# A broadcast through TensorE without a diagonal, and two conversion steps placed anew, in a fused decoder layer

## The chip, the cores and the metric

The kernel runs on one core of one Trainium2 chip. The metric is the time of one execution on the device in microseconds (us), taken as the median of several runs.

A core has five engines with a queue of instructions each: TensorE (PE, matrix products, with PEld for its weight loads), VectorE (DVE), ScalarE (ACT), GpSimd (POOL) and SyncE (SP), which here only issues transfers. They wait for each other by semaphores. Products are summed in PSUM; all other tiles lie in SBUF.

## The reference

One layer of a decoder, with x of 1024 positions by 1024 features, all in float32:

```python
h = rmsnorm(x)
q, k, v, su, sv, g_a, g_b = split(h @ w_in)
y_att = sliding_window_attention(q, k, v, ...)     # window 128, 8 heads of 64, ALiBi, sinks
y_sgu = chunked_spatial_gating(su, sv, ...)
x = x + (sigmoid(g_a) * (y_att @ w_oa) + sigmoid(g_b) * (y_sgu @ w_ob)) @ w_out
x = x + down(silu(conv_g) * conv_v)                # conv over positions of up(rmsnorm(x)), d_ff 2816
```

Two places matter here: the factor 1/rms of each position that the two `rmsnorm` of whole rows need (`rmsnorm(y)` is y times 1/sqrt(mean(y*y) + 1e-6), times a gain).

## The kernel before

Activations are held transposed: features on the 128 partitions, the 1024 positions along a row. So 1/rms differs from column to column, and to multiply by it the kernel needs a tile `rstd_b` of 128 x 1024, in which every partition holds the same 1024 numbers.

*High and low parts.* Most products use a faster form of float32 that keeps fewer bits. Each operand is split: a high part (rounded copy, on ACT, line L75) and a low part (operand minus high part, a subtraction on DVE or POOL), and each product is three: high by high, high by low, low by high. The names end in h and l, or have index 0 and 1.

*Blocks.* From the gates on, a product of 1024 x 1024 operands is put together from seven products of half-size blocks (a Strassen-like scheme). Left blocks (weights) are A11, A12, S1, S2, S3, S4, A22; right blocks (activations) are B11, B21, B22, T1, T2, T3, T4. `prod(o, l, r)` issues the 12 matrix products of one block product (L1014). The sums of weights for S2 and S4 are made on POOL into `lr` (`sums_r`, L608) and split by `split_r` into a tile named AX, the high part on ACT and the low part on POOL (L974).

*Order.* In the stages around the change each engine executes in the order in which the code issues (`manual_schedule`); nothing is reordered. An instruction that waits holds up all behind it on its engine.

*The first place* (L297 to L403, some 30 to 54 us into the run). Behind the k and v projection, `p_ssq` sums the squares of the columns, `rsqrt_cols` turns them into `rstd` (128 x 8: eight columns of 128 positions each; scale and offset on DVE, L115, then a power on POOL, L116). A diagonal tile `diag` is built on DVE from `ident` and `rstd` (L322). Later `rms_rows` multiplies ones (as weights) by the diagonal on PE (L123), which leaves each position's factor in all 128 partitions, and ACT copies the result into `rstd_b` (L125). It is called for the two halves one after the other, between the products of the q projection. Beside this, POOL takes two more powers (`krs`, L116), DVE makes `kr` (L331) and PE transposes it (L338).

*The second place* (L1432 to L1552, some 556 to 601 us). Here the gated MLP begins. `first_pair` computes the first of 22 pairs of column blocks of `up`, and the second pair's first product (`fast_pair(1)`) is interleaved. The last output tile has just been finished, so the sum of squares of the new x is completed here too: `late_split` makes the high and low parts of T2 (low on DVE) and of T4 (low on POOL, both L1445), ACT squares the last tile (L1459), DVE adds these to `sq2` (L1460), and `ssq_cols` lets PE sum the columns (L1340), and makes of them the ratio of the new 1/rms to the one that the activations were already multiplied by (L1344 to L1347, the power on POOL, L116). A diagonal of the ratio is built on DVE (L1349). Meanwhile PE does A22·T4 of the first pair and A11·B11 of the second. Then `rms()` issues the products with the diagonal (L123) and the copies into `rstd_b` (L125), and scales the first pair. The copy `x1` of A11·B11 (named x1f in the profile, L1509) must be taken before A12·B21 is added to the same accumulator.

Of the kernel before, what the change touches and what calls it, by code (L numbers as in the profile page):

```python
# [10 lines left out]
F = mybir.dt.float32  # L11
# [3 lines left out]
ALU = mybir.AluOpType  # L15
# [26 lines left out]
def body(ctx, tc, nc, a):  # L42
    L, H = slice(0, 512), slice(512, 1024)
# [6 lines left out]
    def nm(s):  # L50
        uid[0] += 1
        return f"{s}_{uid[0]}"
# [8 lines left out]
    def PS(s):  # L61
        pools_ = psum["P"]
        pools_.append(pools_.pop(0))
        return pools_[-1].tile([128, 1024], F, tag="P", name=nm(s))

    def PH(s):
        if psum.get("H") is None:
            return PS(s)[:, 0:512]
        return psum["H"].tile([128, 512], F, tag="H", name=nm(s))
# [4 lines left out]
    def copy_hi(dst, src, scale=1.0):  # L74
        return nc.scalar.activation(dst, src, AF.Copy, scale=scale)  # L75
# [26 lines left out]
    ident = base.tile([128, 128], F, name="ident")  # L102
    ones = base.tile([128, 128], F, name="ones")
    mh05 = base.tile([128, 16], F, name="mh05")
    rstd_b = base.tile([128, 1024], F, name="rstd_b")
    rstd = base.tile([128, 8], F, name="rstd")
# [6 lines left out]
    def rsqrt_cols(dst, ss, n, width):  # L113

        nc.vector.tensor_scalar(dst, ss, 1.0 / width, EPS, op0=ALU.mult, op1=ALU.add)  # L115
        return nc.gpsimd.tensor_tensor(dst, dst, mh05[:, :n], op=ALU.pow)  # L116

    msk = base.tile([128, 4, 128], U8, name="msk")

    def rms_rows(pb, diag, hs=(0, 1)):  # L120

        for h, p in zip(hs, pb):
            nc.tensor.matmul(p, ones, diag[:, h * 4:(h + 1) * 4, :], start=True, stop=True)  # L123
        for h, p in zip(hs, pb):
            nc.scalar.copy(rstd_b[:, h * 512:(h + 1) * 512], p)  # L125

# [48 lines left out]
    pa = pa_cm.__enter__()  # L175
# [30 lines left out]
    for k in range(8):  # L206
# [8 lines left out]
        for s in range(8):  # L215
            o = pkv[s // 4][:, (s % 4) * 256:(s % 4 + 1) * 256]
            c = slice(s * 128, (s + 1) * 128)
# [25 lines left out]
    def q_proj(n):  # L243
        half, b = divmod(n, 8)
        w = wq[half]
        p = PH("pq")[:, 0:256]
        c = slice(b * 128, (b + 1) * 128)
        for k in range(8):
            mm3(p, hx(0, k, c), hx(1, k, c), w[:, 0, k, :], w[:, 1, k, :], k == 0, k == 7)
        st[("pq", n)] = p  # L250


    def q_sq(n):
        p = st.pop(("pq", n)).rearrange("p (h d) -> p h d", d=64)
        sq = qp.tile([128, 4, 64], F, tag="qsq", name=nm("qsq"), bufs=2)
        nc.scalar.activation(sq, p, AF.Square)
        st[("q", n)] = [p, sq]
# [42 lines left out]
    for s in range(8):  # L300
        nc.tensor.matmul(p_ssq[:, 2 * s:2 * s + 2], sqsum[:, s * 128:(s + 1) * 128], ones[:, 0:2],
                         start=True, stop=True)
# [9 lines left out]
    for h in range(2):  # L312
# [5 lines left out]
    nc.vector.tensor_tensor(kss3, kss3, rstd2.unsqueeze(2).to_broadcast([128, 8, 2]), op=ALU.mult)  # L318
    rsqrt_cols(krs[:, 0:8], kss[:, 0:8], 8, 64)
    rsqrt_cols(krs[:, 8:16], kss[:, 8:16], 8, 64)  # L320
    diag = pa.tile([128, 8, 128], F, tag="sq", name="diag")
    nc.vector.tensor_tensor(diag, ident.unsqueeze(1).to_broadcast([128, 8, 128]),  # L322
                            rstd.unsqueeze(2).to_broadcast([128, 8, 128]), op=ALU.mult)
    q_sq(0)
    q_sq(1)

# [60 lines left out]
    q_split(0)  # L387
    q_trans(1)
    q_split(1)
    rms_rows([PH("rb")], diag, (0,))  # L390
    q_proj(3)
    k_trans(1)
    rms_rows([PH("rb")], diag, (1,))
    q_sq(2)
    v_split()
    q_ms(2)
# [320 lines left out]
    rb = sg.tile([128, 512], F, name="rb")  # L717
# [620 lines left out]
    def ssq_cols(p):  # L1338
        for s in range(8):
            nc.tensor.matmul(p[:, 2 * s:2 * s + 2], pools["sq2"][:, s * 128:(s + 1) * 128], ones[:, 0:2],  # L1340
                             start=True, stop=True)
        pool = pools["fp"]
        ss = pool.tile([128, 8], F, name="ss8b")
        nc.vector.tensor_copy(ss, p[:, 0:16].rearrange("p (s two) -> p s two", two=2)[:, :, 0])  # L1344
        rsqrt_cols(ss, ss, 8, D)
        nc.vector.reciprocal(rstd, rstd)
        nc.vector.tensor_tensor(ss, ss, rstd, op=ALU.mult)  # L1347
        diag = pool.tile([128, 8, 128], F, tag="ac", name="diag2", bufs=2)
        nc.vector.tensor_tensor(diag, ident.unsqueeze(1).to_broadcast([128, 8, 128]),  # L1349
                                ss.unsqueeze(2).to_broadcast([128, 8, 128]), op=ALU.mult)  # L1350
        return diag

    class Pair(Blocks):

# [66 lines left out]
    lefts = [Left(a["wup"][2 * i], a["wup"][2 * i + 1], i) for i in U_ORDER]  # L1421
# [10 lines left out]
    def first_pair():  # L1432
        w, nx = lefts[0], lefts[1]
        z = PS("pz"), PS("pz")
        q, q2 = Pair(0, w.w, z[::-1]), Pair(1, nx.w)
        xu = pools["fp"].tile([128, 1024], F, tag="h", name="xu", bufs=2)
        x7, u2 = xu[:, L], xu[:, H]
        x1 = pools["fp"].tile([128, 512], F, tag="ac", name="x1", bufs=2)

        def late_split(n, r, eng):  # L1440
            comb[n] = Y(n, R, [128, 2, 4, 512])
            for k in range(0, 4, 2):
                src, h = pools[r][:, k:k + 2, :], comb[n][:, 0, k:k + 2, :]
                copy_hi(h, src)
                eng.tensor_tensor(comb[n][:, 1, k:k + 2, :], src, h.bitcast(F), op=ALU.subtract)  # L1445

        q.prod(q.v1, "A11", "B11")
        nc.scalar.copy(x1, q.v1)
        w.split_r(0)
        nx.load_p()  # L1450
        q.prod(q.g0, "A12", "B21")
        late_split("T2", "raw2", nc.vector)
        nx.load_q()
        nx.load_s3()
        q.prod(q.g1, "S1", "T1")
        nc.scalar.copy(u2, q.g1)
        late_split("T4", "raw4", nc.gpsimd)
        for c, p in zip((L, H), late["px"]):
            nc.scalar.activation(p, late["ac"][:, c], AF.Square)  # L1459
            nc.vector.tensor_tensor(pools["sq2"][:, c], pools["sq2"][:, c], p, op=ALU.add)  # L1460
        q.prod(q.v0, "S3", "T3")
        nc.scalar.copy(x7, q.v0)
        nx.split_p()
        nx.split_s3()
        nc.vector.tensor_tensor(x7, x7, u2, op=ALU.add)
        q.prod(q.g1, "S4", "B22", more=True)
        nc.vector.tensor_tensor(q.g0, q.g0, x1, op=ALU.add)
        q.prod(q.v1, "S2", "T2", more=True)
        pb = q2.zv
        diag = ssq_cols(pb)  # L1470
        nx.sums_r()
        nx.split_q()
        lefts[2].load_p()
        q.prod(q.v0, "A22", "T4", more=True)
        nc.scalar.copy(u2, q.v1)
        q.u2 = u2
        nx.split_r(1)
        nc.vector.tensor_tensor(q.v1, u2, x7, op=ALU.add)
        nc.vector.tensor_tensor(q.v0, u2, q.v0, op=ALU.add)

        def rms():

            rms_rows([pb[:, L], pb[:, H]], diag)
            q.scale(q.zv)
            q.last_sum()

        pools["ft_cm"] = tc.tile_pool(name="ft", bufs=1, reuse_waits="tile")
        return q, q2, rms

    def fast_pair(n, prev, q, hooks, rms=None):  # L1490

        nx = lefts[n + 1] if n + 1 < NPAIR else None

        def temp(t, p="ft"):
            return pools[p].tile([128, 512], F, tag=t, name=nm(t), bufs=2 if p == "ft" else 1)

        if rms:
            x1 = temp("x1f", "wx")
        else:
            prev.last_sum()  # L1500
            prev.tap_v()
            x1, x7, q.u2 = temp("x1"), temp("x7"), temp("u2")
        q.prod(q.g0, "A11", "B11")
        if nx:
            nx.load_q()
            nx.load_s3()
        else:
            hooks[2]()
        nc.scalar.copy(x1, q.g0)  # L1509
        if rms:  # L1510
            rms()
            pools["fp_cm"].__exit__(None, None, None)
            pools["ft"] = pools["ft_cm"].__enter__()
            x7, q.u2 = temp("x7"), temp("u2")
            prev.tap_v()
            q.prod(q.g0, "A12", "B21", more=True)
        prev.tap_g()
        prev.conv()
        q.prod(q.v0, "S3", "T3")
        if nx:  # L1520
            nx.split_s3()
        nc.scalar.copy(x7, q.v0)
        if not rms:
            q.prod(q.g0, "A12", "B21", more=True)
        if rms:
            nx.split_p()
        prev.tanh()
        if not rms:
            prev.gated()
        q.prod(q.g1, "S1", "T1")  # L1530
        if nx and not rms:
            nx.split_p()
        nc.vector.tensor_tensor(x7, x7, q.g1, op=ALU.add)
        if rms:
            prev.gated()
        prev.stores()
        if nx:
            nx.sums_r()
        if n + 2 < NPAIR:
            lefts[n + 2].load_p()  # L1540
        q.prod(q.v0, "A22", "T4", more=True)
        if nx:
            nx.split_q()
            nx.split_r(n + 1)
        else:
            hooks[0]()
        q.prod(q.v1, "S2", "T2")
        q.sums(x1, x7, q.v0)
        if not nx:
            hooks[1]()  # L1550
        q.prod(q.g1, "S4", "B22", more=True)
        return q  # L1552
# [282 lines left out]
```

## Time and profile before

| | us |
|---|---|
| Median of 3 runs | 1198.88 |
| Lowest, highest | 1198.02, 1199.2 |
| Profiled execution, from its first to its last instruction | 1196.2 |
| Median above that span | 2.7 |

| Engine | Busy, share of the span |
|---|---|
| PE | 99% |
| DVE | 74% |
| POOL | 48% |
| ACT | 45% |

A row of a timeline or of the chain has the start in us from the begin of the span, the duration, the engine, the line, the operation, the tiles written and read, shapes and a count; in brackets how long the engine had been idle before, and what ended that. Durations include the time in which an instruction that had been started was held up. For the profiled execution the profile gives its span, and what lies around it is taken as the difference to the median. The mean granted clock of PE was 0.999 of full speed.

### The profile page before, as it was taken

To read this page: it belongs to the slowest core of one execution; us is meant where nothing else is said; L and a number is where in the kernel's file an instruction comes from. 1 tells how busy PE (TensorE), PEld (TensorE's weight loads), DVE (VectorE), ACT (ScalarE), POOL (GpSimd) and SP (SyncE) were. 2 spreads that over 40 slices of the span, in tenths; PEclk is the share of its full clock that TensorE was granted. 3 is DMA by queue.
4 is the path that set the end of the run, shared out by engine and by line. 5 is a ranking of instruction groups with operands and counts; after the bars stand their busy time and mean duration, and the time that the engine had idled before them with its cause. 6 is when DMAs were issued, how large, how long until landed. Compare 5 with 4: busy or idle time off the path is not lost.

```text
span 1196.2 us, 15840 instructions
## 1 busy us (share of the span) xinstructions
PE 1183.4 (99%) x5866; PEld 1002.4 (84%) x5866; DVE 881.4 (74%) x1028; ACT 543.0 (45%) x832; POOL 574.4 (48%) x365
## 2 busy tenths in 40 slices
PE   9999999999999999999999999999999999999998
PEld 9889989988888888888788888888888888888886
DVE  8788975755638565668887788878788788775674
ACT  8555567644335222234444444444444445434331
POOL 2467685588668222344866575656657541000000
PEclk9999999999999999999999999999999999999999
DMA  7010143037786997342143342423333268975471
GB/s 283 23 53 19 54 139 126 11 122 271 237 308 206 358 320 273 128 166 98 45 150 108 104 136 102 149 89 123 109 129 124 87 205 290 370 235 194 150 238 61
DMA packets 79133, 191.27 MB, mean 160 GB/s; under 512 B 8912, under 2 KB 9168, under 8 KB 79056
## 3 DMA queue, kind: packets, MB, share of 16 engines
q1 hardware_dynamic: 79056, 190.26, 46.2%
q8 instruction: 46, 0.75, 0.3%
q14 instruction: 31, 0.25, 0.1%
HBM read 139.63 MB, written 50.59 MB: 159 GB/s over the span
## 4 chain that ended last, share of the span: by engine, by line
PE 82%; DVE 7%; ACT 4%; POOL 3%; DMA 2%; issue 2%; SPq 0%; ACTq 0%; POOLq 0%; DVEq 0%
PE pz L1014 42%; PE pd L1661 10%; PE pdy L1661 8%; PE po L80 2%; PE po L79 2%; PE po L81 2%; PE px L79 2%; PE px L80 2%; PE px L81 2%; DMA ls<-wup 1%; PE pvs L81 1%; PE pvs L79 1%; PE pvs L80 1%; ACT x L75 1%; PE pq L79 1%
## 5 line engine op out<-in xcount | busy, mean ns | idle before, releaser
L1014 PE MATMUL pz<-T,qh 128*128 128x512 f32 x472 | 145.6, 390 | 0.0
L1014 PE MATMUL pz<-B,ph 128*128 128x512 f32 x352 | 108.5, 389 | 0.7 <-ACT x1f L1509 0.7
L974 POOL TENSOR_TENSOR pl<-lp,ph 128x1024 fp32r<-128x1024 f32 x30 | 72.5, 2418 | 75.4 <-ACT ph L75 75.3
L1014 PEld LDWEIGHTS pz<-T,qh 128*128 128x128 f32 x472 | 88.4, 188 | 18.6 <-ACT u L865 0.3
L1014 PE MATMUL pz<-T,ql 128*128 128x512 f32 x236 | 91.8, 389 | 0.0
L96 POOL TENSOR_TENSOR wjl<-wj,wjh 128x512 fp32r<-128x512 f32 (+1 forms) x24 | 40.6, 1693 | 95.7 <-ACT wjh L75 95.7
L974 POOL TENSOR_TENSOR ql<-lq,qh 128x1024 fp32r<-128x1024 f32 x30 | 77.9, 2597 | 9.1 <-ACT qh L75 9.1
L1014 PEld LDWEIGHTS pz<-B,ph 128*128 128x128 f32 x352 | 66.0, 188 | 15.2 <-ACT x1f L1509 1.5
L1030 DVE TENSOR_TENSOR pz<-pz,rstd_b 128x1024 f32<-128x1024 f32 x60 | 73.9, 1232 | 3.3 <-ACT rstd_b L125 1.3
L974 POOL TENSOR_TENSOR s3l<-s,s3h 128x512 fp32r<-128x512 f32 x29 | 38.5, 1328 | 73.4 <-ACT s3h L75 73.4
L1014 PE MATMUL pz<-T,s3h 128*128 128x512 f32 x232 | 71.7, 390 | 0.0
L1014 PE MATMUL pz<-B,pl 128*128 128x512 f32 x176 | 68.5, 389 | 0.0
L1661 PE MATMUL pd<-bl,ah 128*128 128x512 f32 x176 | 68.5, 389 | 0.0
L1661 PE MATMUL pd<-bh,al 128*128 128x512 f32 x176 | 68.5, 389 | 0.0
L1661 PE MATMUL pd<-bh,ah 128*128 128x512 f32 x176 | 68.5, 389 | 0.0
L75 ACT ACTIVATE qh<-lq 128x1024 fp32r<-128x1024 f32 x30 | 31.8, 1061 | 72.0 <-POOL pl L974 36.6
L1014 PE MATMUL pz<-T,AX 128*128 128x512 f32 x264 | 63.4, 389 | 0.0
L1014 PE MATMUL pz<-B,AX 128*128 128x512 f32 x264 | 63.4, 389 | 0.0
L1014 PEld LDWEIGHTS pz<-T,AX 128*128 128x128 f32 x264 | 49.5, 188 | 10.3
L1014 PEld LDWEIGHTS pz<-B,AX 128*128 128x128 f32 x264 | 49.5, 188 | 10.3
L1367 DVE SCALAR_TENSOR_TENSOR tg<-pz,cp,tg 128x1023 f32<-128x1023 f32 (+1 forms) x44 | 56.2, 1278 | 0.8
L1367 DVE SCALAR_TENSOR_TENSOR tv<-pz,cp,tv 128x1023 f32<-128x1023 f32 (+1 forms) x44 | 56.2, 1277 | 0.8
(343 smaller groups left out, 3549.6 us busy)
## 6 DMA issues: line engine op xcount, KB each, us to landing
ls<-wup SPq DMA_DIRECT2D x22, 512.0 KB, 5.7
sum<-ls SPq DMA_DIRECT2D x22, 512.0 KB, 5.1
lp<-wup SPq DMA_DIRECT2D x22, 512.0 KB, 3.5
ra<-wdown SPq DMA_DIRECT2D x44, 256.0 KB, 4.8
b<-T SPq DMA_DIRECT2D x44, 256.0 KB, 3.8
B<-tv SPq DMA_DIRECT2D x33, 256.0 KB, 2.0
T<-tt SPq DMA_DIRECT2D x33, 256.0 KB, 2.1
b<-B SPq DMA_DIRECT2D x33, 256.0 KB, 3.5
```

The source lines that it names most:

```text
L75: return nc.scalar.activation(dst, src, AF.Copy, scale=scale)
L79: nc.tensor.matmul(out, wh, mh, start=first, stop=False, **kw)
L80: nc.tensor.matmul(out, wh, ml, start=False, stop=False, **kw)
L81: nc.tensor.matmul(out, wl, mh, start=False, stop=last, **kw)
L96: nc.gpsimd.tensor_tensor(l[:, :nk, :], r[:, :nk, :], h[:, :nk, :].bitcast(F), op=ALU.subtract)
L974: nc.gpsimd.tensor_tensor(l, r, h.bitcast(F), op=ALU.subtract)
L1014: nc.tensor.matmul(o, p[:, k, :], y[:, q, k, :], start=not more and k == 0 and j == 0, stop=k == 3 and j == 2, skip_group_check=True)
L1030: nc.vector.tensor_tensor(z, z, rstd_b, op=ALU.mult)
L1367: nc.vector.scalar_tensor_tensor(t[:, j:], p[:, 0:1024 - j], cw[:, ci, 2 - j:3 - j], t[:, j:], op0=ALU.mult, op1=ALU.add)
L1661: nc.tensor.matmul(o[d], p[:, k - k0, m], q[:, k - k0, :], start=new and k == 0 and j == 0, stop=k == HK - 1 and j == 2, skip_group_check= ...
```

## The change

Three edits. The diagonals go: `rms_rows` takes the 128 x 8 tile itself and, for each of its eight columns, multiplies the column, repeated 128 times as weights, by the identity, which also leaves the 128 factors in every partition. T4's low parts move from POOL to DVE, behind T2's. The split of the second pair's AX (`split_r`) moves from `first_pair` to behind `rms()` in `fast_pair(1)`; on ACT its high part now follows the copies of `x1` and of `rstd_b`, on POOL its low part keeps its place. Otherwise each engine's order stays.

```diff
-    def rms_rows(pb, diag, hs=(0, 1)):
+    def rms_rows(pb, col, hs=(0, 1)):
         for h, p in zip(hs, pb):
-            nc.tensor.matmul(p, ones, diag[:, h * 4:(h + 1) * 4, :], start=True, stop=True)
+            for s in range(4):
+                c = 4 * h + s
+                nc.tensor.matmul(p[:, s * 128:(s + 1) * 128], col[:, c:c + 1].to_broadcast([128, 128]), ident,
+                                 start=True, stop=True)
...
-    diag = pa.tile([128, 8, 128], F, tag="sq", name="diag")
-    nc.vector.tensor_tensor(diag, ident.unsqueeze(1).to_broadcast([128, 8, 128]),
-                            rstd.unsqueeze(2).to_broadcast([128, 8, 128]), op=ALU.mult)
...
-    rms_rows([PH("rb")], diag, (0,))
+    rms_rows([PH("rb")], rstd, (0,))
...
-    rms_rows([PH("rb")], diag, (1,))
+    rms_rows([PH("rb")], rstd, (1,))
...
-        diag = pool.tile([128, 8, 128], F, tag="ac", name="diag2", bufs=2)
-        nc.vector.tensor_tensor(diag, ident.unsqueeze(1).to_broadcast([128, 8, 128]),
-                                ss.unsqueeze(2).to_broadcast([128, 8, 128]), op=ALU.mult)
-        return diag
+        return ss
...
-        late_split("T4", "raw4", nc.gpsimd)
+        late_split("T4", "raw4", nc.vector)
...
         q.u2 = u2
-        nx.split_r(1)
...
-            rms_rows([pb[:, L], pb[:, H]], diag)
+            rms_rows([pb[:, L], pb[:, H]], ratio)
...
         if rms:
             rms()
+            lefts[n].split_r(n)
```

More of the change, by code (lines that the diff above doesn't have):

```diff
@@ L1469, in first_pair @@
         pb = q2.zv
-        diag = ssq_cols(pb)
+        ratio = ssq_cols(pb)
         nx.sums_r()
```

## The prediction

> **What bounds the kernel now.** I read the page first (busy time, chain of work), then the waits of TensorE (PE), then the chain in order of time, and last the engines' timelines around the two places that the diff touches.
>
> ```profile
> span 1196.2 us, 15840 instructions
> PE 1183.4 (99%) x5866; PEld 1002.4 (84%) x5866; DVE 881.4 (74%) x1028; ACT 543.0 (45%) x832; POOL 574.4 (48%) x365
> PE pz L123 <- DVE diag L1349: 1.6, 1, 1.6
> PE pz L1014 <- ACT x1f L1509: 0.7, 1, 0.7
> PE pk L338 <- DVE kr L331: 0.6, 1, 0.6
> 584.58 397.41 PE pz L1014 x1752
> ```
>
> PE is busy for 99% of the span, and from 584.58 the chain is nothing but PE products back to back, until the last columns at 1189. So a change pays exactly what it does to PE's start at 584.58, if nothing later goes short. Two of PE's longest waits stand right in front of that moment and belong to the lines changed: 1.6 us for the diagonal (L1349) and 0.7 us for the copy x1f (L1509). A third, 0.6 us for kr at L338, stands just behind the first diagonal (L322).
>
> **The second place, around 580 us.** PE's rows, then ScalarE (ACT), then VectorE (DVE) and GpSimd (POOL):
>
> ```profile
> 579.93 0.39 PE L1014 MATMUL pz<-B,pl 128*128 128x512 f32 x1
> 581.90 1.98 PE L123 MATMUL pz<-diag,ones 128*128 128x512 f32 x4 [1.58 <-DVE diag L1349]
> 584.58 0.73 PE L1014 MATMUL pz<-B,ph 128*128 128x512 f32 x2 [0.70 <-ACT x1f L1509]
> 578.42 0.57 ACT L1475 COPY xu<-pz 128x512 f32<-128x512 f32 x1
> 583.00 1.06 ACT L75 ACTIVATE AX<-lr 128x1024 fp32r<-128x1024 f32 x1 [4.01 <-POOL lr L608]
> 583.96 0.57 ACT L1509 COPY x1f<-pz 128x512 f32<-128x512 f32 x1
> 584.43 1.08 ACT L125 COPY rstd_b<-pz 128x512 f32<-128x512 f32 x2
> 577.65 1.65 POOL L116 TENSOR_TENSOR ss8b<-ss8b,mh 128x8 f32<-128x8 f32 x1
> 579.28 1.28 POOL L608 TENSOR_TENSOR lr<-lq,lp 128x512 f32<-128x512 f32 x1
> 579.34 1.25 DVE L1347 TENSOR_TENSOR ss8b<-ss8b,rstd 128x8 f32<-128x8 f32 x1 [2.75 <-POOL ss8b L116]
> 580.62 1.23 DVE L1349 TENSOR_TENSOR diag<-ident,ss8b 128x1024 f32<-128x1024 f32 x1
> 580.64 2.33 POOL L608 TENSOR_TENSOR lr<-lp,lr 128x512 f32<-128x512 f32 x1
> ```
>
> PE's last product of A11·B11 starts at 579.93 and ends at 580.32; with the usual 0.227 from start to start (397.41/1752) its next instruction could start at 580.16. It starts at 581.90, because the eight ratios (L1347) are there only at 580.59 and the diagonal behind them takes 1.23. After the four passes (to 583.88) PE waits again, for x1f. That copy needs only A11·B11, done at 580.32, but in ACT's order it is queued behind the split of AX, which waits for POOL's second lr (to 582.97).
>
> The edits, one by one:
>
> *AX's split issued later.* x1f follows the copy that ends at 578.99, so it runs from about 580.36 to 580.93. It is wanted only when the rstd products are through, near 582.0, so the 0.70 goes. AX's high part now stands behind the two rstd_b copies: 1.06 us, about 583.3 to 584.4, while DVE multiplies by rstd_b over 1024 columns (the diagonal's like took 1.23), so the tap behind it on ACT finds ACT free. AX's low part on POOL takes 2.41 and would be done near 586.9; its first reader is the fifth of the following products (12 × 0.227 = 2.72 each), about 593. No transfer is issued inside that step, and no other queue's order changes. Cost nothing; cover six us.
>
> ```profile
> 585.70 2.41 POOL L974 TENSOR_TENSOR AX<-lr,AX 128x1024 fp32r<-128x1024 f32 x1
> ```
>
> *No second diagonal.* 1.23 us of DVE between ratio and products goes. What is late next is the ratio itself, so the third edit decides.
>
> *T4's low parts from POOL to DVE.* The rows of this stretch, and one low part (L239) that no POOL work disturbed:
>
> ```profile
> 30.53 1.21 DVE L239 TENSOR_TENSOR u0l<-wu,u0h 128x1024 fp32r<-128x1024 f32 x1
> 564.17 2.81 POOL L974 TENSOR_TENSOR AX<-lr,AX 128x1024 fp32r<-128x1024 f32 x1 [3.45 <-ACT AX L75]
> 565.07 2.99 DVE L1445 TENSOR_TENSOR T<-T2f,T 128x1024 fp32r<-128x1024 f32 x1 [0.36 <-ACT T L75]
> 567.50 2.83 POOL L1445 TENSOR_TENSOR T<-T4f,T 128x1024 fp32r<-128x1024 f32 x1 [0.52 <-ACT T L75]
> 567.99 3.42 DVE L1445 TENSOR_TENSOR T<-T2f,T 128x1024 fp32r<-128x1024 f32 x1
> 571.33 1.27 DVE L1460 TENSOR_TENSOR sq<-sq,px 128x512 f32<-128x512 f32 x2
> 572.87 1.84 PE L1340 MATMUL pz<-ones,sq 128*128 128x2 f32 x16
> 573.61 2.85 POOL L974 TENSOR_TENSOR pl<-lp,ph 128x1024 fp32r<-128x1024 f32 x1
> 569.78 1.06 ACT L75 ACTIVATE ph<-lp 128x1024 fp32r<-128x1024 f32 x1
> 574.95 1.53 DVE L115 TENSOR_SCALAR ss8b<-ss8b 128x8 f32<-128x8 f32 x1
> ```
>
> The rows read like two engines taking turns: DVE's first T2 part starts at 565.07 but ends 1.08 after POOL's AX (566.98); POOL's first T4 part ends 2.27 after that; DVE's second T2 part ends 1.08 after POOL's (570.33). An instruction that both reads and writes on-chip memory waits for the other engine's to finish, then takes 1.1 on DVE or 2.3 on POOL. The 128x8 step L1347 shows it at its barest: 1.25 us, ending with POOL's 579.28 + 1.28.
>
> The Trainium skill ("SBUF — State Buffer", Who interferes with whom) states this as a lock: a VectorE instruction with two SBUF inputs and a GpSimd one that reads SBUF exclude each other, and whichever issues first holds on to its end. The turns above agree; by this rule a low part moved to DVE is cheap only while POOL has nothing, and POOL's next work must not get in ahead of it.
>
> Played forward without POOL's two T4 parts: first T2 part to 568.06, second to 569.2 (POOL is idle), T4's two to 570.3 and 571.4. POOL's next work, pl, needs ph, ready at 570.84, so the last T4 part starts some 0.6 us ahead of it and pl waits until 571.4, then runs to 573.7 (now 576.46). The squares' sum follows at 571.4 to 572.6, where it stands today, and PE's L1340 doesn't move. POOL's s3l, half as wide (1.28, as lr), follows behind one DVE step and ends about 575.4; L115, today held until 576.48 by pl, ends near 575.5; the power of 1.65 ends near 577.2; L1347, held once by the first lr (1.28), ends near 578.5. That is 1.7 us ahead of PE's 580.16.
>
> *Eight products of 128 columns for two of 512.* Each float32 product appears as two passes, so 16 passes, each with its own weight load, replace 4. No row shows a repeated column as weights. Bounds: L1340's 16 passes with 2 columns go from 572.87 to the next product's start at 574.57,
>
> ```profile
> 574.57 0.72 PE L1014 MATMUL pz<-T,qh 128*128 128x512 f32 x2
> 48.66 0.86 PE rb L123 x2
> 1.05 3.36 PE L204 MATMUL warm<-ones 128*128 128x128 f32 x14 [1.05 <-POOL mh L108]
> L204 PEld LDWEIGHTS warm<-ones x14: 288/333/337, 1.0 to 3.8; 128*128 128x128 f32 x14
> L1340 PEld LDWEIGHTS pz<-ones,sq x16: 187/192/192, 572.6 to 574.4; 128*128 128x128 f32 x16
> ```
>
> or 0.106 each, bound by the load. Two 512-column passes take 0.86 at L123's first place, 0.43 each, a quarter of which is 0.11. So 0.106 to 0.115 if load and multiplication overlap, as everywhere in this trace. The form itself, 128x128 float32, is shown by L204 alone: 3.36/14 = 0.24 each, in the first microseconds. I take 0.115, because L204's loads too last 333 ns where the same load lasts 192 at 573 us: that row is slow all over. Sixteen passes make 1.84, against 1.98.
>
> The Trainium skill ("TensorE: Matmul & The Clock Gate", What's actually happening) says that PE runs at half clock until some 3.4 us of work. By it L204's 0.24 is 0.12 warm and the sixteen passes 1.92; read without it they are 3.84 (a rival below). The trace's doubled load time agrees.
>
> Sum: 580.16 + 1.84 = 582.0 for the start now at 584.58: **2.55 us** gained. Next late is the copy of rstd_b: products end near 582.2, copies near 583.3; the product that overwrites their source starts at 582.0 + 2.72 = 584.7, so 1.4 us to spare.
>
> **The first place, around 37 us.**
>
> ```profile
> 33.27 1.65 POOL rstd L116
> 35.50 1.22 DVE L322 TENSOR_TENSOR diag<-ident,rstd 128x1024 f32<-128x1024 f32 x1
> 35.61 2.62 POOL krs L116
> 38.46 0.70 DVE kr L331
> 38.34 0.28 PE L81 MATMUL pq<-wq,x 128*128 128x256 f32 x1
> 38.66 0.38 ACT L256 ACTIVATE qsq<-pq 128x256 f32<-128x256 f32 x1 [2.49 <-PE pq L81]
> ```
>
> The same power costs 1.65 and 2.62: the second began 0.1 after the diagonal, and waited for it. Without L322 it ends 0.97 earlier, kr at 38.2 instead of 39.16, and PE, whose last product starts at 38.34, need not stop for its 0.58. DVE's queue behind kr still waits for the second qsq at 39.04, so I count no more than 0.58. Eight passes per half cost 8 × 0.115 = 0.92 for 0.86, twice: −0.1. **0.5 us**; from 0 (the attention stages behind it alternate among all engines and may swallow it) to 0.75.
>
> Together 3.05 us. The profiled execution spans 1196.2, so its span should be 1193.15; the median of the runs, 1198.88, lies 2.7 above that span, taken as unchanged: 1195.8.
>
> **The rivals.**
>
> *Passes at L204's price, 0.24.* Second place 3.84, start at 584.0, gain 0.6; at the first place 3.84 for 1.72, half of it beside PE's waits there, less the 0.58: minus 0.5 to 1.5. About 1199.3, no change that can be told. Against: loads of 192 ns and 0.106 spacing wherever PE is under way.
>
> *Slower: T4's low parts hold up the squares.* DVE's queue now has them ahead of L1460. If they cost what the T2 parts show now (2.99 and 3.42) behind a second T2 part at 571.4, the first square is in at 578.4, not 572.0; PE's L1340 starts at 578.4 instead of 572.64, and 5.8 lost against 3.05 won gives 1201.6. It decides from 3.05 us of delay on; if only pl slips ahead of the last T4 part, the delay is 2.4 and the time 1198.2. Against: those durations are POOL's turns, and POOL has nothing between 566.98 and 570.84.
>
> *The ratio is still late.* If POOL's pl or s3l come as late as today, L1347 ends at 580.6 rather than 578.5; PE waits 0.4 to 1.5, the change only shortens the wait: 1196.3 to 1197.4.
>
> *First place without yield.* Its 0.5 is swallowed in the attention stages: 1196.3.
>
> **How the numbers follow.** A measurement of this kernel can tell about 0.2%, 2.4 us, from no change, so the line is at 1196.5. Forecast 0.70, nearly all beyond that line (0.67 faster, 0.03 same); no yield at the first place 0.12 (0.07 and 0.05); late ratio 0.05 and passes at double price 0.06, both the same; squares held up 0.07, slower. Faster 0.74, same 0.19, slower 0.07. The range goes from 1194.9 (0.75 at the first place, 2.7 at the second, and half a microsecond of the runs' spread) up to 1198.0, which takes in the late ratio and leaves out the slow squares and the doubled passes.
>
> **What would show it.** In the profile after: PE's wait for DVE before L123's successor gone, L1014 following the ratio's products with no wait for x1f; two T4 parts on DVE of about 1.2 each before 571.5; L1340 still at 572.6 less the shift from the first place; the power krs at 1.65; 16 passes within 1.9 us. The forecast is wrong if L1340 starts late, if the passes stand more than 0.2 apart, or if PE waits anew between 585 and 982.

## The result, and the profile after

The changed kernel takes 1195.45 us (median of 6 runs, 1194.99 to 1196.68) beside 1199.04 us for the kernel before (6 runs): a ratio of 0.9971, 95% interval 0.9960 to 0.9982, so 3.6 us or 0.3% less. Run again beside the last experiments it took 1195.54 beside 1198.63: 0.9972, 0.9961 to 0.9984.

The page of the changed kernel, span and busy times, then the chain:

```profile
span 1195.0 us, 15884 instructions
PE 1183.7 (99%) x5890; PEld 1003.3 (84%) x5890; DVE 879.7 (74%) x1028; ACT 541.7 (45%) x832; POOL 566.7 (47%) x363
PE 87%; DVE 6%; DMA 2%; issue 2%; POOL 1%; ACT 1%; SPq 0%; ACTq 0%; POOLq 0%; DVEq 0%
```

This span is that of the slowest of the six runs (1196.68 us; the others span 1193.3 to 1194.8). Its waits of PE, in us in total, times and longest, tell why:

```profile
PE pkv L79 <- ACT x L75: 1.8, 2, 1.7
PE warm L207 <- POOL mh L108: 1.1, 1, 1.1
PE pv L501 <- POOL cl L488: 0.7, 1, 0.7
PE pqt L278 <- DVE krs L329: 0.6, 1, 0.6
```

The 1.7 us belong to the second load of x near 8 us, far ahead of anything changed; run again, the kernel showed 0.9 there. The three waits that the prediction was about (diagonal, x1f, kr) are gone, and no wait of PE between 560 and 600 us has come in their place.

The timeline of the second place after the change, PE, then ACT, DVE and POOL:

```profile
573.12 1.84 PE L1340 MATMUL pz<-ones,sq 128*128 128x2 f32 x16
580.18 0.39 PE L1014 MATMUL pz<-B,pl 128*128 128x512 f32 x1
580.41 1.95 PE L125 MATMUL pz<-ident,ss8b 128*128 128x128 f32 x16
582.11 0.71 PE L1014 MATMUL pz<-B,ph 128*128 128x512 f32 x2
582.66 0.39 PE L1014 MATMUL pz<-B,pl 128*128 128x512 f32 x1
580.61 0.58 ACT L1505 COPY x1f<-pz 128x512 f32<-128x512 f32 x1 [1.36 <-PE pz L1014]
582.39 1.07 ACT L128 COPY rstd_b<-pz 128x512 f32<-128x512 f32 x2 [1.20 <-PE pz L125]
583.35 1.07 ACT L75 ACTIVATE AX<-lr 128x1024 fp32r<-128x1024 f32 x1
569.38 2.35 DVE L1442 TENSOR_TENSOR T<-T4f,T 128x1024 fp32r<-128x1024 f32 x2
571.65 1.27 DVE L1457 TENSOR_TENSOR sq<-sq,px 128x512 f32<-128x512 f32 x2
577.46 1.26 DVE L1347 TENSOR_TENSOR ss8b<-ss8b,rstd 128x8 f32<-128x8 f32 x1 [1.66 <-POOL ss8b L116]
571.18 2.80 POOL L974 TENSOR_TENSOR pl<-lp,ph 128x1024 fp32r<-128x1024 f32 x1 [3.95 <-ACT ph L75]
580.03 2.81 POOL L974 TENSOR_TENSOR ql<-lq,qh 128x1024 fp32r<-128x1024 f32 x1
```

PE runs from A11·B11's last product into the sixteen passes and from them into A12·B21 without a bracket: no wait. From the start of that last product (580.18) to the start of A12·B21 (582.11) it is 1.93 us, where it was 4.65 (579.93 to 584.58). I call this the distance; 2.72 us of it are gone. T4's two low parts take 2.35 on DVE, the squares follow in time, and the ratio is there at 578.72, 1.7 us before PE asks for it.

The first place, in the timelines of POOL and PE after the change (of the two powers, the first belongs to the half that `kr` waits for):

```profile
36.86 3.24 POOL L116 TENSOR_TENSOR krs<-krs,mh 128x8 f32<-128x8 f32 x2 [0.70 <-DVE krs L115]
39.73 0.60 PE L338 MATMUL pk<-ident,kr 128*128 128x128 f32 x4
49.03 1.06 PE L125 MATMUL rb<-ident,rstd 128*128 128x128 f32 x8
49.84 0.48 PE L422 MATMUL sc<-kTh,qs 128*128 128x256 f32 x2
```

The two powers take 3.24 us together, 1.6 each, L338 follows with no wait, and eight passes take 0.81 us (49.03 to 49.84). Comparing the starts of the same products in the two traces: PE lags the trace of before by 1.26 us ahead of this place (the late x) and by 0.57 behind it, so it gained 0.69 here.

So the two places gave 3.4 us. But the lead that PE has over the trace of before where that one shows 584.58 (2.47, with the late start in it) is 1.78 at 968 us and 1.2 from 1011 to the end. In the second trace of the changed kernel it is 3.12, then 2.41 at 932, 2.36 at 968 and 2.32 at the end, so some 0.7 is lost each time on the way to 968, and the 0.6 around 1010 only once. The loss can be seen in the waits of PE's weight loads between 600 and 968 us, of which the kernel before has none:

```profile
PEld pz L1014 <- ACT x L1505: 1.8, 9, 0.2
```

### The profile page after: what moved, and what is told of

Its sections match the earlier page's. It is cut to its first block, busy times and chain, and to the rows that moved or that the text cites. A ratio compares the mean times of both kernels' runs of the same rounds, so it can differ in the third digit from the quotient of the medians.

```text
span 1195.0 us, 15884 instructions
## 1 busy us (share of the span) xinstructions
PE 1183.7 (99%) x5890; PEld 1003.3 (84%) x5890; DVE 879.7 (74%) x1028; ACT 541.7 (45%) x832; POOL 566.7 (47%) x363
## 4 chain that ended last, share of the span: by engine, by line
PE 87%; DVE 6%; DMA 2%; issue 2%; POOL 1%; ACT 1%; SPq 0%; ACTq 0%; POOLq 0%; DVEq 0%
PE pz L1014 46%; PE pdy L1658 8%; PE pd L1658 7%; PE px L80 2%; PE po L81 2%; PE po L80 2%; PE px L81 2%; PE px L79 2%; PE po L79 2%; PE pvs L79 1%; PE pvs L80 1%; PE pvs L81 1%; PE pq L79 1%; DMA ls<-wup 1%; PE pq L81 1%
## 5 line engine op out<-in xcount | busy, mean ns | idle before, releaser
L974 POOL TENSOR_TENSOR AX<-lr,AX 128x1024 fp32r<-128x1024 f32 x22 | 53.7, 2442 | 5.1 <-ACT AX L75 5.1
```

The source lines that it names most:

```text
L974: nc.gpsimd.tensor_tensor(l, r, h.bitcast(F), op=ALU.subtract)
```

## The experiments

The theory: the diagonal and the copy x1f stood in a row in front of PE at 580 us, the ratio right behind them, and T4's move to DVE is what brings the ratio in time; the diagonal at 35 us held up POOL's power. The rivals: one edit alone gives it all; the first place yields nothing; T4's low parts are cheap on DVE for another reason than POOL's idleness. All medians and ratios below are against the kernel before, run on the same chip beside each group; edits are shown against the changed kernel.

| Kernel | Median, us | Before, us | Ratio, 95% interval | Distance, us |
|---|---|---|---|---|
| products only | 1196.74 | 1198.60 | 0.9983 (0.9974 to 0.9991) | 4.02 |
| AX later only | 1197.74 | 1198.60 | 0.9992 (0.9984 to 1.0001) | 3.41 |
| T4 only | 1196.12 | 1198.60 | 0.9980 (0.9969 to 0.9990) | 2.56 |
| AX later in all pairs | 1194.22 | 1198.60 | 0.9961 (0.9948 to 0.9974) | 1.93 |
| T4 on POOL | 1196.90 | 1197.96 | 0.9987 (0.9979 to 0.9996) | 2.51 |
| POOL kept busy | 1204.91 | 1197.96 | 1.0057 (1.0044 to 1.0071) | 1.93 |
| POOL memsets | 1194.63 | 1197.96 | 0.9974 (0.9963 to 0.9985) | 1.93 |
| AX later, q first | 1193.56 | 1197.96 | 0.9962 (0.9949 to 0.9974) | 1.93 |
| change again | 1195.54 | 1198.63 | 0.9972 (0.9961 to 0.9984) | 1.93 |
| AX later, again | 1194.88 | 1198.63 | 0.9964 (0.9950 to 0.9977) | 1.93 |
| T4 on POOL, again | 1196.72 | 1198.63 | 0.9981 (0.9972 to 0.9990) | 2.55 |
| first diagonal kept | 1196.41 | 1198.63 | 0.9978 (0.9969 to 0.9987) | 1.93 |

### One edit at a time

**Products only** (T4's low parts on POOL and AX's split early, as before):

```diff
-        late_split("T4", "raw4", nc.vector)
+        late_split("T4", "raw4", nc.gpsimd)
...
+        nx.split_r(1)
...
-            lefts[n].split_r(n)
```

> The eight products in place of the diagonal at both places; T4's low parts stay on POOL and AX's split stays ahead of the copy x1f. Measure: the distance from the start of the last product of A11.B11 to the first of A12.B21; 4.65 us before, 1.93 us with all three edits. My theory (ratio late because of POOL's turns, x1f late because of AX): the products start when the ratio is there, 0.7 us after PE is free (with the diagonal 1.7 us); POOL's second lr is no longer held by the diagonal and ends near 581.9, AX to 583.0, x1f to 583.5: distance 3.6, PE waits for x1f at its end. Together with 0.6 at the first place the run gains 1.6. Rival (AX does not hold x1f up; the diagonal alone was the wait): distance 2.4 to 2.7, a gain of 2.6 or more.

Its timeline at the second place:

```profile
579.08 2.05 PE L125 MATMUL pz<-ident,ss8b 128*128 128x128 f32 x16 [0.34 <-DVE ss8b L1347]
582.37 0.73 PE L1014 MATMUL pz<-B,ph 128*128 128x512 f32 x2 [1.24 <-ACT x1f L1506]
```

The diagonal's wait of 1.6 has shrunk to 0.34, but the wait for x1f has grown from 0.70 to 1.24: distance 4.02, 0.63 gained. x1f is held by AX's split ahead of it on ACT; what is won in front of it is mostly lost to it. The 4.02 are 0.4 over the theory's 3.6: POOL's second sum of weights, for which AX waits, still takes 1.68 where an undisturbed one takes 1.28.

**AX's split later only** (diagonals kept at both places, T4 on POOL):

```diff
-            for s in range(4):
-                c = 4 * h + s
-                nc.tensor.matmul(p[:, s * 128:(s + 1) * 128], col[:, c:c + 1].to_broadcast([128, 128]), ident,
-                                 start=True, stop=True)
+            nc.tensor.matmul(p, ones, diag[:, h * 4:(h + 1) * 4, :], start=True, stop=True)
...
-        late_split("T4", "raw4", nc.vector)
+        late_split("T4", "raw4", nc.gpsimd)
```

> Only AX's split moved behind the copies of rstd_b; diagonals and T4 as before. My theory: x1f is in long before the diagonal's passes are through, so only the 0.7 us behind them goes: distance 3.7 to 3.95 for 4.65, gain 0.7 to 0.9; no gain at the first place. Rival (something else than AX holds the following product): distance stays 4.65, no gain.

Distance 3.41, which is 1.24 less, but not all of that is gained. The diagonal is still waited for, and A12·B21 now starts right behind the start of the last wide pass, at 582.78. Its third product follows only 0.85 later, where this takes 0.55 in the changed kernel (582.11 to 582.66). The trace of this kernel, then of before:

```profile
581.36 1.98 PE L123 MATMUL pz<-diag,ones 128*128 128x512 f32 x4 [1.60 <-DVE diag L1349]
582.78 1.02 PE L1014 MATMUL pz<-B,ph 128*128 128x512 f32 x2
583.63 0.39 PE L1014 MATMUL pz<-B,pl 128*128 128x512 f32 x1
```

```profile
585.16 0.39 PE L1014 MATMUL pz<-B,pl 128*128 128x512 f32 x1
```

Up to this third product the distance is 4.26 here and 5.23 before (579.93 to 585.16): 0.97 gained, still more than the bracket of 0.70 that the trace of before puts down to x1f. In the other kernels the two ways of measuring a gain agree within 0.03. By the same measure, from the first pass to the third product, the four wide passes take 2.27 (581.36 to 583.63) and the sixteen narrow ones 2.25 in the changed kernel (580.41 to 582.66), or 2.37 where they follow a wait as the wide ones do here (T4 on POOL, 580.23 to 582.60). So the narrow form is no cheaper than the wide one, and hardly dearer. The time, 0.9 us less by medians, can't be told from no change (the interval reaches 1).

**T4's low parts on DVE only** (diagonals kept, AX early):

```diff
-            lefts[n].split_r(n)
...
+        nx.split_r(1)
...
+        diag = pool.tile([128, 8, 128], F, tag="ac", name="diag2", bufs=2)
+        nc.vector.tensor_tensor(diag, ident.unsqueeze(1).to_broadcast([128, 8, 128]),
+                                ss.unsqueeze(2).to_broadcast([128, 8, 128]), op=ALU.mult)
```

> Only T4's low parts moved to DVE; diagonals and AX's split as before. My theory: the ratio comes near 578.5 for 580.6; behind it the diagonal and POOL's second lr contend for the turn, diagonal at 580.0 to 581.0; x1f, behind AX and lr, at 581.4 to 582.8: distance 2.7 to 2.9, gain 1.8 to 1.9, the most of any single edit, though on its face it only moves work from a 48% engine to a 74% one. Rival (the low parts hold up the squares on DVE): PE waits in front of the column sums by 2 us or more, distance from there unchanged, run slower than before.

Distance 2.56: this edit alone takes 2.09 of the 2.72 us. It brings the ratio forward, so even the diagonal is ready in time, and POOL's two sums of weights too, so AX and x1f come earlier. Singly the edits save 0.63, 0.97 (up to the third product) and 2.09, together 2.72: they shorten the same wait.

### T4 back on POOL

```diff
-        late_split("T4", "raw4", nc.vector)
+        late_split("T4", "raw4", nc.gpsimd)
```

> The change without its T4 edit: products without a diagonal, AX's split late, T4's low parts on POOL again. By T4 alone the distance from the last product of A11.B11 to the first of A12.B21 fell from 4.65 to 2.56, by 2.1; with all three edits it is 1.93. My theory (one queue of waits, shared by the edits): the ratio is then 0.5 to 0.7 late for a PE that is free, the passes take 1.8 and x1f is in: distance 2.4 to 2.5, only 0.5 more than with the whole change, and the run 0.5 slower than with it. Rival (the edits add up): 1.93 + 2.1, distance 4.0, run 2 us slower than with the whole change.

The distance, 2.51, is as expected: PE waits 0.32 for the ratio. But the time is well over that: the trace had a new wait of 1.6 us for ACT's copy L1519 at 590 us. It could be chance, so it ran again beside the changed kernel.

> T4's low parts back on GpSimd, the rest of the change kept, again. Theory A: the 1.6 us wait for ACT's x at 590 us (its chain begins at a load of a sum that landed 5.7 us after its issue, 3.3 in the changed kernel) was a transfer that came late by chance; then it is absent this time and the kernel is 0.3 to 0.6 us slower than the changed one, the 0.32 us wait for the ratio alone. Theory B: the load comes late each time, because GpSimd's low part of q ends 1.4 us later and holds the buffer; then the wait of 1 to 2 us is there again, and the kernel is 1.2 to 2.0 us slower than the changed one.

It isn't chance. PE's waits between 560 and 600 us in the second trace:

```profile
PE pz L1014 <- ACT x L1519: 1.1, 1, 1.1
PE pz L125 <- DVE ss8b L1347: 0.4, 1, 0.4
```

and where the first comes from, in the timelines of ACT, and of SP's queue, which issues the next pair's transfers:

```profile
589.99 0.63 ACT L75 ACTIVATE s3h<-s 128x512 fp32r<-128x512 f32 x1 [2.64 <-DMA s<-sum]
590.52 0.57 ACT L1519 COPY x<-pz 128x512 f32<-128x512 f32 x1
581.51 0.33 SPq L85 DMA_DIRECT2D lp<-wup  x1
583.88 0.32 SPq L928 DMA_DIRECT2D lq<-sum  x1
584.79 0.36 SPq L933 DMA_DIRECT2D s<-sum  x1
```

The same two issues in the changed kernel beside it:

```profile
582.21 0.32 SPq L928 DMA_DIRECT2D lq<-sum  x1
583.12 0.36 SPq L933 DMA_DIRECT2D s<-sum  x1
```

SP waits for POOL: lp's buffer comes free with the second lr, lq's with POOL's ql, and the sum for S3 is queued behind both. With T4 on POOL they go out 1.7 us later, and the transfer of s then takes 5.1 us to land (3.6 in the changed kernel). ACT sits in front of its split and the copy L1519 queues behind it. The median is 1.2 us over the changed kernel's, the lower edge of theory B, and its chain is the one that the trace shows. By the starts of PE's products the second place costs 0.6 more than with the whole change and the wait at 590 us 1.4 (1.9 in the first trace), while the 0.8 that the changed kernel gives back from there to the end is not given back here: 1.2 together. Moving T4's low parts was worth something at a place that the prediction did not look at: it lets the next pair's loads go out earlier, and PE, now 2.7 us earlier, needs them so. Why the later transfer also takes 1.5 longer to land stays open.

### POOL given something else to do

Do T4's low parts cost 1.1 us on DVE because POOL is idle? Two subtractions on POOL at T4's former place, their result unused:

```diff
+        late["h"] = h
...
+        spare = late["h"].rearrange("p (k c) -> p k c", c=512)
+        for _ in range(2):
+            nc.gpsimd.tensor_tensor(spare, pools["raw2"][:, 0:2, :], pools["raw2"][:, 2:4, :], op=ALU.subtract)
```

> The whole change, and in the place on POOL that T4's low parts left, two subtractions of 128x1024 between tiles in SBUF that nobody reads (added work, its result unused). My theory (DVE and POOL take turns): the T2 and T4 low parts on DVE each wait for one POOL step, the first square's sum ends some 6.0 us later, PE stands in front of the column sums for 6 us and everything behind shifts: 1201.4, slower than before by 2.5. That is the forecast's slower rival made to happen. By the Trainium skill (TensorE: Matmul & The Clock Gate, What is actually happening) so long a stand may also halve PE's clock for some 3.4 us, up to 1.7 more. Rival (long low parts in the trace before had another cause, such as DVE reading T2 slowly): no stand, time as with the change alone.

and four fills instead, which write the same tile and read nothing:

```diff
+        for _ in range(4):
+            nc.gpsimd.memset(spare, 0.0)
```

> As the kernel with POOL kept busy, but POOL's steps in that place are four memsets of 128x1024 (about 0.95 us each by the 64x1024 ones at the start of the run), which write and read nothing. If the turns are about reading on-chip memory, as the Trainium skill says (SBUF - State Buffer, Who interferes with whom), the low parts on DVE stay at 1.1 to 1.2 us while POOL is busy, PE does not stand, and the time is that of the change alone within 0.5 us. If any work of POOL blocks them, each waits for a memset: T4's second low part ends up to 4 us later, PE stands 3 to 4 us, time near 1199.

With subtractions, DVE, POOL and PE:

```profile
570.55 6.68 DVE L1443 TENSOR_TENSOR T<-T4f,T 128x1024 fp32r<-128x1024 f32 x2
577.15 1.27 DVE L1461 TENSOR_TENSOR sq<-sq,px 128x512 f32<-128x512 f32 x2
566.15 6.72 POOL L1458 TENSOR_TENSOR h<-T2f 128x1024 f32<-128x1024 f32 x2
577.88 3.58 PE L1341 MATMUL pz<-ones,sq 128*128 128x2 f32 x16 [5.62 <-DVE sq L1461]
```

With fills:

```profile
567.74 2.35 DVE L1443 TENSOR_TENSOR T<-T4f,T 128x1024 fp32r<-128x1024 f32 x2
565.53 4.01 POOL L1458 MEMSET h<- 128x1024 f32 x4
```

POOL is busy next to DVE in both. The low parts take 3.34 us each beside subtractions and 1.18 beside fills, and the time of the second is that of the change (1194.63, ratios overlap). So what holds up DVE is POOL's reading, not its being busy. The Trainium skill ("SBUF — State Buffer", Who interferes with whom) says just this: a VectorE instruction with two SBUF inputs contends with a GpSimd one that reads SBUF, not with one that only writes it. Both traces agree.

The busy kernel also prices the prediction's slow rival, and it is dearer than I worked out: 1204.91, not 1201.4, and 6.95 over the kernel before of its chip, where 2.5 were expected. PE waits 5.6 us for the squares as expected, but the granted clock then falls. Busy times by stretch of that kernel (PE, PEld, DVE, ACT, POOL, then the granted clock, the DMA share and GB/s):

```profile
572.00:576.00 4.00, 0.26 (x2) 0.00 (x0) 4.00 (x2) 0.00 (x0) 4.00 (x2) 0.99 0.00 0
578.00:580.00 2.00, 2.00 (x10) 2.00 (x11) 1.64 (x3) 0.00 (x0) 0.36 (x1) 0.50 0.00 0
584.00:586.00 2.00, 2.00 (x6) 1.58 (x5) 0.88 (x1) 0.00 (x0) 1.92 (x2) 0.50 0.00 0
586.00:588.00 2.00, 2.00 (x9) 1.57 (x9) 0.03 (x1) 1.53 (x2) 0.66 (x2) 0.96 0.22 47
```

PE's last product before the stop ends at 572.3. At 575.9, 3.7 us later, PE is granted half the clock, and it keeps half until 586.2, though it works again from 577.9 on. Up to 581.3 that work is L1341's passes of two columns; from there, for 4.8 us, it is products of 512 columns. Comparing starts with the changed kernel's trace, PE lags by 5.8 us more at L1341's start than in the products before it and by 9.8 after 586: the slow clock costs 4.0. The Trainium skill ("TensorE: Matmul & The Clock Gate", What's actually happening) gives at least one window of about 3.4 us for each of the two steps, down after an idle window and up after a busy one, with windows that run on freely. The fall agrees. The rise agrees only if passes of two columns don't count as busy: windows of 3.4 counted on from 575.9 end at 579.3, 582.7 and 586.2, and the third is the first that is filled with products of 512 columns. No run here tests that reading.

### The first place alone

```diff
+    diag = pa.tile([128, 8, 128], F, tag="sq", name="diag")
+    nc.vector.tensor_tensor(diag, ident.unsqueeze(1).to_broadcast([128, 8, 128]),
+                            rstd.unsqueeze(2).to_broadcast([128, 8, 128]), op=ALU.mult)
...
-    rms_rows([PH("rb")], rstd, (0,))
+    rms_diag(PH("rb"), 0)
```

(and the second half the same way; `rms_diag` is the former product of ones with the diagonal, and the copy.)

> The change with the diagonal kept at the first place (near 37 us) and its two products of 512 columns there; all of the second place as changed. Theory: the 0.58 us wait for kr and the long second power (2.6 instead of 1.64 us) are back, and the kernel is 0.5 to 0.75 us slower than the change alone. Rival: the attention stages swallow the gain; then TensorE's start at 60 us is the same within 0.2 us and so is the time.

```profile
35.75 4.22 POOL L116 TENSOR_TENSOR krs<-krs,mh 128x8 f32<-128x8 f32 x2 [0.70 <-DVE krs L115]
39.36 0.66 PE L345 MATMUL pk<-ident,kr 128*128 128x128 f32 x4 [0.59 <-DVE kr L338]
```

The two powers take 4.22 us instead of 3.24 and the wait for kr is back. By the starts of the same products this kernel is 0.74 us ahead of the changed one before this place and 0.03 behind it, so the first diagonal costs 0.71. By medians it is 0.87 slower; the profiled run has a wait of 0.8 us at 368 us that the changed kernel's beside it has not, and which comes and goes from run to run, so I take the 0.71. The attention stages swallow nothing. Whether they even add to the gain stays open: of the four traces with the first diagonal three have this wait (0.5, 0.8 and 1.8 us), of the ten without it one (0.2).

### Where the lead goes again

After the second place the pairs run in a loop over DVE (sums and taps), ACT (splits, copies), POOL (sums and low parts). Reading the changed kernel's timeline at a pair shows ACT:

```profile
635.65 1.06 ACT L75 ACTIVATE AX<-lr 128x1024 fp32r<-128x1024 f32 x1 [3.35 <-POOL lr L608]
636.62 0.57 ACT L1024 COPY u<-pz 128x512 f32<-128x512 f32 x1
```

The copy u, which DVE's sums need, could go 1.8 us before (DVE is done with its source at 634.84), but is queued behind AX's split, which waits for POOL: the same knot that the change undid for the second pair alone. Undoing it in the other pairs:

```diff
             nx.split_q()
-            nx.split_r(n + 1)
...
         q.sums(x1, x7, q.v0)
+        if nx:
+            nx.split_r(n + 1)
```

> All three edits, and in the pairs behind the second one AX's split is moved behind the copy u in the same way (on ACT u, then AX's high part, for AX, then u). In the profile after, PE starts the MLP 2.47 us earlier than before but is only 1.75 us ahead at its last pair and 1.2 at the end; every second pair its weight load waits 0.2 for the copy x, and on ACT u waits behind AX, which waits for POOL's lr. My theory: a loop through DVE, ACT and POOL with a period a little over PE's own catches up with PE; u ahead of AX shortens the loop by 1 to 2 us in each pair, these waits go, and the run is 0.5 to 1.2 us faster than with the change alone, 4.0 to 4.8 faster than before. Rival (the loss is jitter of one execution or the transfers of the last stage): the same time as the change alone within 0.3.

> The changed kernel with AX's split issued later in the other pairs as well, beside the changed kernel on one chip. Theory: the loop of VectorE, ScalarE and GpSimd in the pairs costs the change 0.7 (to 968 us) to 1.3 us (to the end), and this order takes it away: 0.7 to 1.3 us faster than the change alone. Rival: the difference of the two earlier medians (1194.2 against 1195.45) was the start-up of the profiled runs and the chips: within 0.4 us of the change alone.

The second trace of it, ACT at the same pair:

```profile
633.23 0.59 ACT L1024 COPY u<-pz 128x512 f32<-128x512 f32 x1 [2.57 <-DVE pz L1023]
634.08 1.06 ACT L75 ACTIVATE AX<-lr 128x1024 fp32r<-128x1024 f32 x1 [0.26 <-POOL lr L608]
```

Against the changed kernel on the same chip, PE is 0.95 us ahead at 590 us, by differences at the start and in the attention, and 1.74 at 966, and the waits of the weight loads between 600 and 968 are gone. Against the kernel before, its lead stays at 4.08 from 584.58 to the end. So the loop cost the change 0.8 us. By medians the gain is 0.66 on one chip (1194.88 beside 1195.54; 0.7 to 1.3 were expected) and 1.2 across two. The direction was the same both times, but the intervals of the ratios overlap: it is the traces that show it.

The change doesn't bring the loop forward as it does PE. DVE's first `tt` behind the second place, first in the trace of before and then of after:

```profile
597.32 0.72 DVE L608 TENSOR_TENSOR tt<-tv 128x512 f32<-128x512 f32 x1
```

```profile
595.28 2.52 DVE L608 TENSOR_TENSOR tt<-tv 128x512 f32<-128x512 f32 x1
594.85 2.40 POOL L974 TENSOR_TENSOR ql<-lq,qh 128x1024 fp32r<-128x1024 f32 x1
```

Two microseconds earlier on DVE, but now POOL's ql reads first, and 1.8 of them go to waiting for the turn. Over all the traces the loss goes with this hold and AX's early place together. Where `tt` takes 2.5 to 3.0 and AX is early (the changed kernel, products only, POOL kept busy, the memsets, first diagonal kept), PE's weight loads wait 1.7 to 2.0 in all between 600 and 968; where it takes 0.7 to 1.3 (before, AX later only, T4 only, T4 on POOL) they don't, and with AX later in all pairs they don't either, though `tt` takes 2.5. So it isn't the size of PE's gain that decides: products only lost all of its 0.6 from the second place again, T4 only kept its 2.1. No run removed this hold alone.

### A step further at the first place

The later order again, and at the first place q's normalization ahead of k's low part, to take away PE's waits for krs and qs there (0.6 and 0.4):

```diff
     q_norm(0)
-    k_lo(0)
     q_norm(1)
-    k_norm(1)
+    k_lo(0)
...
     q_split(1)
+    k_norm(1)
```

> The kernel with AX's split later in all pairs, and at the first place two steps of DVE's queue set anew: the second q_norm ahead of kTl's low parts, and krs/kr of the second half behind the four low parts of qs (kr's reader comes 4 us later). With the diagonal gone PE there waits 0.56 for the second qr and 0.40 for qs; DVE is busy without a break between. My theory: both waits go or nearly so, 0.5 to 0.8 us, with waits for kTl at most 0.2 in their place; the run is 0.5 faster than with AX later alone, near 1193.7. Rival (the attention stages give it back): same as with AX later alone.

Of the two waits one new one of 0.5 was left (for k's low part, which frees the bank of the first products), and PE gained 0.53 between 42 and 60 us against the later order alone. The ratio is the same as without (0.9962 and 0.9961), so a gain in time isn't shown. The kernels with the later order have the lowest ratios of all, 0.9961 to 0.9964 (1193.6 to 1194.9 us).

## Why the prediction was right, point by point

The forecast was 1195.8 us; 1195.45 and 1195.54 were measured. The mechanism is the one named. That the number came so close is in part luck: two waits were worth more than they were taken for, the passes saved less, and a loss behind 600 us was not seen; these make up for each other.

- **Second place, forecast 2.55 (2.58 by its own terms, 584.58 less 582.0), measured 2.72, or 2.75 up to the third product.** All its steps came within 0.3 us of their times: T4's low parts to 571.7 (571.4), the ratio at 578.7 (578.5), A12·B21 at 582.11 (582.0), in a trace that runs 0.25 us later there. The diagonal's wait was right: PE free at 580.16, passes from 581.90. The passes' saving was mis-sized: they were to save 0.14 (1.84 for 1.98) and save next to nothing (2.25 against 2.27, as shown under AX's split). A pass takes 0.11 (from 580.41 the fourteenth starts at 581.86), within the two bounds, so sixteen take about 1.8; but the 1.98 of the four wide ones is a row that runs on to the last pass's modelled end, and at the 0.43 that the prediction read off the first place they make 1.72.
- **Passes at 0.24.** Wrong: a column repeated as weights goes at 0.11, like L1340's passes of two columns, so the number of columns doesn't set this pace. (L204's loads last 1.7 times as long as L1340's, 333 ns for 192, not double.)
- **x1f's wait.** Gone, but it was mis-sized the other way: the bracket says 0.70, its removal alone gave 0.97. The bracket counts from the modelled end of the last wide pass, and the first two products behind the wait take 0.58 (584.58 to 585.16), where two take 0.45 at the usual pace.
- **First place, forecast 0.5, measured 0.69 and 0.71.** The wait went whole, and it too was worth more than its bracket of 0.58: PE lags by 1.26 at the last product ahead of L338 (38.34 before, 39.60 after) and by 0.47 at the first one behind it (39.61 and 40.08), so 0.79 is gained there. Of this 0.07 is lost again at 43 to 44 us, where the wait for krs (L278) is 0.56 for 0.48, and 0.03 at the second half's eight passes; I had put 0.1 for the passes of both halves. The rival in which the attention stages swallow the gain is refuted by the kernel with the first diagonal kept.
- **T4 on DVE delays the squares.** Not here, and the lock is why: with POOL reading, the parts take 3.34 each and PE stops for 5.6 us. The rival was right as a mechanism and underpriced by some 4 us (2.7 over the kernel before given, 6.95 measured), which is what the slow clock behind the stop cost (4.0).
- **"No transfer is issued inside that step".** True of AX's split, but the prediction didn't follow the move of T4's parts into POOL's queue and from there to SP's. It should have: the next pair's loads are released by POOL's lr and ql, and had they stayed as late as with T4 on POOL, 1.4 to 1.9 us would have been lost at 590 us.
- **"The forecast is wrong if ... PE waits anew between 585 and 982".** It does, by little: the weight loads wait in every second pair, and 0.7 to 0.8 of the 3.4 us is given back there. The prediction followed the path up to 593 us and took the lead from there on as kept; it had no step for whether DVE, ACT and POOL follow.
- **The time around the span.** I took 2.7 us as lying around it. Each run's own time is 1.7 above its span (1196.68 and 1195.0; 1195.56 and 1193.8), so the profiled execution of before took about 1197.9, a microsecond under its median. Since the sum was made as a difference to the median, the error cancelled.

So 3.05 us were forecast, and the traces give 3.4 less 0.7 to 0.8, or 2.6 to 2.7; the medians say 3.6 and 3.1. The gap between those is within the runs' spread: runs of the kernel before on one chip lie up to 5.1 us apart (1196.86 to 1202.0), and in the traces the wait at 8 us comes to 1.7 and the one at 368 us to anything from 0 to 1.8.

## What to carry to other kernels

When several waits stand in a row in front of the engine that sets the end, each edit alone gets little, and the edit that brings all of them forward, here two subtractions moved to another engine, gets most; ask what each is late for, not only how long it is waited for. Follow the work that is moved into the queue that it leaves: what stood behind it there now releases its buffers and starts its transfers earlier, and that can be worth as much as the wait removed. A microsecond gained by the bounding engine lasts only if the loop of the other engines comes forward with it; look for a copy that others need queued behind one that waits. In these traces the idle time in a row's bracket is the least that a wait costs: 0.70 and 0.58 were worth 0.97 and 0.79. And measure a gain at the second or third instruction behind a wait, since the first can start while the one ahead of it still holds the engine.

## What the hardware showed that I had not expected

- A column of 128 x 8, repeated 128 times as weights, goes at 0.11 us from pass to pass at 128 columns, as close as passes of two columns.
- A pause of PE of 5.6 us cost 4.0 more: 3.7 us into it the granted clock fell to 0.50, and it stayed there for 10.2 us, the last 4.8 of them with products of 512 columns.
- A subtraction of 128x1024 on DVE costs 1.18 us beside a POOL that fills and 3.34 beside one that subtracts; a step of 128x512 at the wrong moment 2.52 instead of 0.72.
- The same transfer of 256 KB, issued 1.7 us later, took 5.1 us to land instead of 3.6, and 5.7 in another run. What held it up was not found.
